# Two down projections, 1024 columns at a time, with seven products instead of eight in four of eleven pairs of chunks

## The chip, the cores and the metric

The kernel runs on one core of a Trainium2 chip. The metric is the device time of one execution in microseconds (us), which is to be low. The kernel before takes 1485.39 us (median of three runs, 1484.65 to 1486.05). All times below come from these runs, from the profile of one execution, or from questions put to that execution's trace.

## What is computed

The reference is one encoder layer over 256 tokens with 2048 features, all in float32. Cut to what matters here:

```python
x = x + merged @ w_out                       # attention branches, before
hf = rms_norm(x, ffn_norm)
g = dwconv_centred(hf @ w_ffn_gate, conv_w, conv_b)
x = x + (gelu(g) * (hf @ w_ffn_up)) @ w_ffn_down     # w_ffn_down: 5632 x 2048
gate_p = sigmoid(rms_norm(x, ple_norm) @ w_ple_gate)
x = x + gate_p * (p @ w_ple_proj)
return rms_norm(x, final_norm)
```

The product with `w_ffn_down` contracts over 5632 features, which are 44 chunks of 128. It is the product that the change touches.

## The kernel before, in words

**Precision.** Every float32 operand is split into a part `hi`, rounded to the matmul's format, and the rest `lo`. A product is three matmuls: hi by hi, hi by lo, lo by hi.

**The stream of weights.** All weights lie in HBM as one stream of blocks of 128x128, packed in the order of their use. A piece is 16 blocks (1 MB). `load` fetches a piece into one of three buffers `raw` by the DMA queue of SyncE (SP). `split_to` makes two splits of 8 blocks out of a piece: ScalarE (ACT) copies 128x1024 numbers of `raw` into `whi`, then VectorE (DVE) subtracts, `wlo` = `raw` - `whi`. There are four buffers of `whi` and four of `wlo`, so the split of a piece waits until TensorE (PE) is through with the split four earlier; the load of a piece waits until the last `wlo` of the piece three earlier is made. Each engine takes its instructions strictly in the order in which a scheduler wrote them.

**The work in order.** `_plan` lists jobs: the input projections (kinds q, k, v) with attention in between, the branch products (ga, gb, ba, bb), the output projection (o), and then, twice, one half of the gated MLP: 22 chunks f of the gate product (g) and the up product (u), followed by the down product (d0, d1) over these 22 chunks. After d1 come the two small products of the per-layer embedding (pp, two chunks each) and the gate of it (pg), and the final norm. The g and u products (`product`, `block`) hold a weight block still and stream the 256 tokens as hi and lo; the others (`wide_product`) hold 128 tokens still and stream 512 columns of weights. A d job in the kernel before is one quarter of the columns (512): for each of the 22 chunks, six matmuls, three for each half of the tokens, into two PSUM banks. `joined` then adds each bank to the residual `x` on DVE, and for d1 ACT takes squares for the next norm. `flip` transposes the residual on PE, 4 transposes per two chunks, and `gained` splits the result into `mov` (the operand `pl` of pg) with one ACT and one DVE instruction per chunk. The jobs pp and pg read what ACT puts into `ph`, and the last gain `lg`, which is fetched by a DMA of 1 MB.

**Work that is placed by a table.** `at` and `run_due` hang steps (flips, norms, fetches) on a job and a chunk number; the scheduler then places them in each engine's queue.

## Time and profile before

| | |
|---|---|
| median of three runs | 1485.39 us (1484.65 to 1486.05) |
| the profiled execution | 1485.03 us |
| its span, first to last instruction | 1483.1 us, so 1.9 us lie around it |
| granted TensorE clock | 0.998 |
| PE busy / DVE busy / ACT busy | 1472.1 / 975.9 / 729.4 us |
| read from HBM | 279.49 MB |

In the rows that follow, PE is TensorE, PEld its loading of the still operand, DVE VectorE, ACT ScalarE, SPq the DMA queue of SyncE. A row of a group has its busy time and the mean length of one instruction (in ns), and behind the bar's second part the idle time before it with what ended it. The timeline's rows have start and length in us, and in brackets how long the engine was idle before and what it waited for. A matmul's length there includes its latency: matmuls follow each other faster than that, so the pace of PE is read from the distance between starts, not from lengths. The same holds in a smaller way for DVE and ACT. d0 runs from 887.7 to 995 us of the span, d1 from 1256 to about 1374 us.

### The profile page before, as it was taken

Reading aid. Unit: us, or ns where it says so; the run is one execution under the profiler, and the core shown is the slowest. Engines: PE = TensorE matmul, PEld = TensorE weight load, DVE = VectorE, ACT = ScalarE, POOL = GpSimd, SP = SyncE. Lnnn points to the kernel's source line nnn. Section 1 sums busy time; section 2 is a strip of 40 time slices with the busy share of each in tenths; the row PEclk is TensorE's granted clock in tenths of the full one; section 3 lists DMA queues with packets and bytes.
Section 4 is the critical chain, followed back from the end, with each engine's and each line's share of the span. In section 5 each row is a group of like instructions: output and inputs, shape, how many; then the busy total and the mean of one; then the engine's idle time right before and its main releaser. Section 6 shows DMA issues by size and latency. Waiting matters only on the chain.

```text
span 1483.1 us, 19449 instructions
## 1 busy us (share of the span) xinstructions
PE 1472.1 (99%) x7618; PEld 1258.2 (85%) x7618; DVE 975.9 (66%) x1406; ACT 729.4 (49%) x1032; POOL 3.7 (0%) x9
## 2 busy tenths in 40 slices
PE   9999999999999999999999999999999999999997
PEld 8888888888888888888888888888888888888886
DVE  7686665655554555578888885447888887555565
ACT  7565444444444444554554554344555555444553
POOL 0000000000000000000000000000000000000000
PEclk9999999999999999999999999999999999999999
DMA  8744444446555555565555555555555555555552
GB/s 320 257 153 161 170 171 172 169 178 205 196 194 205 184 203 202 178 220 183 188 197 188 183 197 197 187 189 193 196 179 194 199 179 191 199 175 193 196 188 99
DMA packets 46375, 282.89 MB, mean 191 GB/s; under 512 B 5124, under 2 KB 9988, under 8 KB 14028
## 3 DMA queue, kind: packets, MB, share of 16 engines
q1 hardware_dynamic: 44268, 277.31, 52.3%
q10 hardware_dynamic: 2016, 4.33, 1.1%
q8 instruction: 60, 0.98, 0.3%
q14 instruction: 31, 0.25, 0.0%
HBM read 279.49 MB, written 2.14 MB: 190 GB/s over the span
## 4 chain that ended last, share of the span: by engine, by line
PE 97%; DVE 1%; ACT 0%; DMA 0%; issue 0%; POOL 0%; ACTq 0%; POOLq 0%; DVEq 0%
PE acc L202 28%; PE acc L225 17%; PE acc L226 17%; PE acc L227 17%; PE acc L203 14%; PE first L202 2%; PE first L203 1%; PE pt L483 0%; PE pt L608 0%; DVE wlo L192 0%; PE sp L442 0%; PE misc L498 0%; PE pt L629 0%; DMA x<-in_xt 0%; PE misc L429 0%; PE misc L430 0%
## 5 line engine op out<-in xcount | busy, mean ns | idle before, releaser
L192 DVE TENSOR_TENSOR wlo<-raw,whi 128x1024 fp32r<-128x1024 f32 (+1 forms) x519 | 632.2, 1218 | 467.3 <-ACT whi L191 465.7
L191 ACT ACTIVATE whi<-raw 128x1024 fp32r<-128x1024 f32 (+1 forms) x519 | 547.9, 1056 | 670.7 <-PE acc L227 355.2
L202 PE MATMUL acc<-mov,whi 128*128 128x512 f32 x1840 | 642.1, 394 | 0.0
L203 PE MATMUL acc<-mov,wlo 128*128 128x256 f32 x1840 | 512.9, 279 | 0.0
L202 PEld LDWEIGHTS acc<-mov,whi 128*128 128x128 f32 x1840 | 344.7, 187 | 77.5
L203 PEld LDWEIGHTS acc<-mov,wlo 128*128 128x128 f32 x1840 | 346.8, 188 | 0.5
L225 PE MATMUL acc<-whi,mov 128*128 128x512 f32 (+1 forms) x640 | 247.6, 387 | 0.0
L227 PE MATMUL acc<-whi,mov 128*128 128x512 f32 (+1 forms) x640 | 246.2, 385 | 0.0
L226 PE MATMUL acc<-wlo,mov 128*128 128x512 f32 (+1 forms) x640 | 246.2, 385 | 0.0
L225 PEld LDWEIGHTS acc<-whi,mov 128*128 128x128 f32 x640 | 120.8, 189 | 24.0 <-DVE wlo L192 0.8
L227 PEld LDWEIGHTS acc<-whi,mov 128*128 128x128 f32 x640 | 120.7, 189 | 24.0
L226 PEld LDWEIGHTS acc<-wlo,mov 128*128 128x128 f32 x640 | 120.8, 189 | 22.9
L225 PE MATMUL acc<-whi,act 128*128 128x512 f32 x352 | 137.5, 391 | 0.0
L227 PE MATMUL acc<-whi,act 128*128 128x512 f32 x352 | 137.0, 389 | 0.0
L226 PE MATMUL acc<-wlo,act 128*128 128x512 f32 x352 | 136.9, 389 | 0.0
L227 PEld LDWEIGHTS acc<-whi,act 128*128 128x128 f32 x352 | 66.1, 188 | 13.9
L225 PEld LDWEIGHTS acc<-whi,act 128*128 128x128 f32 x352 | 66.1, 188 | 13.6
L226 PEld LDWEIGHTS acc<-wlo,act 128*128 128x128 f32 x352 | 66.1, 188 | 13.2
L253 ACT ACTIVATE t<-acc 128x256 f32<-128x256 f32 x115 | 42.1, 366 | 0.0
L257 DVE TENSOR_TENSOR u<-acc,t 128x256 f32<-128x256 f32 x100 | 41.8, 418 | 0.0
L202 PE MATMUL first<-mov,whi 128*128 128x512 f32 x112 | 38.6, 397 | 0.2
L225 PE MATMUL acc<-whi,yab 128*128 128x512 f32 x96 | 37.3, 389 | 0.0
(144 smaller groups left out, 912.5 us busy)
## 6 DMA issues: line engine op xcount, KB each, us to landing
raw<-in_wts SPq DMA_DIRECT2D x251, 1024.0 KB, 4.8
raw<-in_wts SPq DMA_DIRECT2D x12, 512.0 KB, 7.2
x<-in_xrows ACTq DMA_DIRECT2D x8, 256.0 KB, 5.3
x<-in_xt SPq DMA_DIRECT2D x13, 128.0 KB, 6.7
mov<-hold SPq DMA_DIRECT2D x3, 514.0 KB, 6.6
mov<-hold SPq DMA_DIRECT2D x2, 768.0 KB, 6.9
mov<-in_last_gain ACTq DMA_DIRECT2D x1, 1024.0 KB, 5.7
out<-x ACTq DMA_DIRECT2D x2, 384.0 KB
```

The source lines that it names most:

```text
L191: nc.scalar.activation(hi, src, AF.Copy)
L192: nc.vector.tensor_tensor(lo, src, hi.bitcast(F32), op=ALU.subtract)
L202: nc.tensor.matmul(acc, hi[:, o, :], m, start=first, stop=False, skip_group_check=True)
L203: nc.tensor.matmul(acc[:, T:], lo[:, o, :], m[:, :T], start=False, stop=last, skip_group_check=True)
L225: nc.tensor.matmul(acc, xh, hi, start=(k == 0), stop=False)
L226: nc.tensor.matmul(acc, xh, lo, start=False, stop=False)
L227: nc.tensor.matmul(acc, xl, hi, start=False, stop=(k == n - 1))
L253: keep(nc.scalar.activation(t, acc[:, T:], AF.Copy, scale=scale))
L257: nc.vector.tensor_tensor(u, acc[:, :T], t, op=ALU.add)
```

## The change

Each half's down product becomes two jobs of 1024 columns instead of four of 512. With 256 tokens (two halves of rows, A1 and A2), two chunks of 128 features and 1024 columns (two halves of 512), a pair of chunks is a 2x2 by 2x2 product of quarters. For four of the eleven pairs (numbers 0 to 3 of `ORDER`, which alternates them with unsaved pairs: 4, 0, 5, 1, 6, 2, 7, 3, 8, 9, 10) the eight products of quarters are replaced by seven products of sums of quarters, in the variant with 15 additions. The other seven pairs are computed as before, into four of the seven banks.

- *Activations.* `add_up`, once per half after chunk 7 of the up product, forms four sums for all four saved pairs (four DVE instructions of 128x512) and splits them (two ACT and two DVE instructions of 128x1024). Chunks 0 to 7 are kept in float32 in `a32` for that.
- *Weights.* For a saved pair, `combine` forms four differences of the weights' quarters from the piece `raw` in the buffer `spare`: one DVE instruction of 128x1024 and two of 128x512. The piece then gives four splits instead of two: 8 blocks of `raw`, 8 of `spare`, 8 of `spare`, 4 of `raw`. The splits serve 6, 6, 6 and 3 matmuls; a split of an unsaved piece serves 12. `seven_product` asks for splits one further ahead than `wide_product`.
- *Spreading.* After the last saved pair, `spread_sums` takes p1 with one ACT instruction and, with eight DVE instructions of 128x512, adds p1, p5, p6 and p7 to the residual in the four places where they belong. p2, p3, p4 and c22 gather the unsaved pairs and are joined at the end of the job as before: four `joined` per job, in a row.
- *Banks.* The seven banks are all that PSUM has but one; the two jobs of a half swap the names, so that a job begins in banks that have long been read.
- *Memory and moves.* The large buffers are cut anew. The last gain is fetched in job pp 2 instead of at the beginning of d1. After the last d1 job, four flips instead of two are left, at pp 1, pp 2 (two) and pp 3.

The diff, cut to its core:

```diff
-        wide("d%d" % half, "w_ffn_down", half * FHALF, FHALF)
+        for c in range(2):
+            jobs.append(("d%d" % half, c, "w_ffn_down", tuple(range(8 * c, 8 * c + 8)), half * FHALF, FHALF))
...
+ORDER = [4, 0, 5, 1, 6, 2, 7, 3, 8, 9, 10]
+SAVED = 4
...
+        if isinstance(n, tuple) and len(n) == 8:
+            for m in ORDER:
+                if m < SAVED:
+                    _SEVEN.add(len(blocks))
+                blocks += [(name, k0 + 2 * m + e, c) for e in range(2) for c in n]
+            continue
...
+def _splits():
+
+    subs = [(int(a), n, None) for a, n in zip(np.cumsum([0, 1, 2, 4, 4]), (1, 2, 4, 4, 5))]
+    for a in range(PIECE, len(_BLOCKS), PIECE):
+        if a in _SEVEN:
+            subs += [(a, PIECE, part) for part in range(4)]
+        else:
+            subs += [(a + o, SUB, None) for o in range(0, PIECE, SUB)]
+    return subs
+
...
+            if part is not None:
+                src = combine(src, part)
+                n = src.shape[1]
...
+    def combine(b, part):
+
+        if part == 0:
+            state["turn"] = turn = 1 - state.get("turn", 1)
+            state["t"] = held["spare"][:, turn * PIECE * P:(turn + 1) * PIECE * P].rearrange("p (b n) -> p b n", n=P)
+            four = b.rearrange("p (q b) n -> p q (b n)", q=4)
+            t13 = state["t"][:, :8, :].rearrange("p (q b) n -> p q (b n)", q=2)
+            nc.vector.tensor_tensor(t13, four[:, 1::2], four[:, :2], op=ALU.subtract)
+            return b[:, 8:, :]
+        if part == 1:
+            t1, t2, t4 = (state["t"][:, c:c + 4, :] for c in (0, 8, 12))
+            nc.vector.tensor_tensor(t2, b[:, 12:, :], t1, op=ALU.subtract)
+            nc.vector.tensor_tensor(t4, b[:, 8:12, :], t2, op=ALU.subtract)
+            return state["t"][:, :8, :]
+        return state["t"][:, 8:, :] if part == 2 else b[:, :4, :]
 
     def block(acc, m, first, last, ahead=3):
...
+    def seven_product(i, still, sums, tags, done):
...
+        seen, uses = {}, {}
+        for m in ORDER:
+            for name in ("p2", "p3", "p4") + (("p1", "p5", "p6", "p7") if m < SAVED else ("p2", "p3", "p4", "c22", "c22")):
+                uses[name] = uses.get(name, 0) + 1
+
+        def step(name, pair, hi, lo):
+            xh, xl = pair
+            seen[name] = e = seen.get(name, 0) + 1
+            acc = of(name)
+            nc.tensor.matmul(acc, xh, hi, start=(e == 1), stop=False)
+            nc.tensor.matmul(acc, xh, lo, start=False, stop=False)
+            nc.tensor.matmul(acc, xl, hi, start=False, stop=(e == uses[name]))
+
...
+        k = 0
+        for m in ORDER:
+            b = state["at"]
+            s, _ = _SUB_OF[b]
+            if m < SAVED:
+                each = ([("p3", sums(m, 3), 0, 4), ("p2", a(2 * m + 1, 0), 0, 0)],
+                        [("p5", sums(m, 0), 1, 0), ("p7", sums(m, 2), 1, 4)],
+                        [("p6", sums(m, 1), 2, 0), ("p4", a(2 * m + 1, 1), 2, 4)],
+                        [("p1", a(2 * m, 0), 3, 0)])
+            else:
+                each = [[(name, a(2 * m + e, t), e, o) for name, t, o in (("p2", 0, 0), ("p3", 0, 4), ("p4", 1, 0),
+                                                                         ("c22", 1, 4))] for e in range(2)]
+            for e, steps in enumerate(each):
+                if m >= SAVED or e % 2 == 0:
+                    run_due(i, k)
+                    k += 1
+                for name, pair, part, o in steps:
+                    split_to(s + part + 4)
+                    hi, lo = (w[:, o:o + 4, :] for w in subs[s + part])
+                    step(name, pair, hi, lo)
+                del subs[s + part]
+            state["at"] = b + PIECE
+            if m == SAVED - 1:
+                done(bank)
+        return bank
 
     sc = ctx.enter_context(tc.tile_pool(name="sc", bufs=2))
 
@@ -334,11 +432,10 @@
...
+            f = n % FHALF
+            v = held["a32"][:, f, :] if f < 2 * SAVED else u
+            nc.vector.tensor_tensor(v, u, held.pop(("gelu", n)), op=ALU.mult)
+            halves(held["act"][:, f, :], v)
+            if f == 2 * SAVED - 1:
+                add_up()
...
+    def add_up():
+
+        a = held["a32"].rearrange("p (m e) (t n) -> p m e t n", e=2, t=2)
+        a11, a12, a21, a22 = a[:, :, 0, 0], a[:, :, 1, 0], a[:, :, 0, 1], a[:, :, 1, 1]
+        s = held["s32"]
+        nc.vector.tensor_tensor(s[:, 0], a21, a22, op=ALU.add)
+        nc.vector.tensor_tensor(s[:, 1], s[:, 0], a11, op=ALU.subtract)
+        nc.vector.tensor_tensor(s[:, 2], a11, a21, op=ALU.subtract)
+        nc.vector.tensor_tensor(s[:, 3], a12, s[:, 1], op=ALU.subtract)
+        hi, lo = held["shl"][:, 0], held["shl"][:, 1]
+        for c in (slice(0, 2), slice(2, 4)):
+            nc.scalar.activation(hi[:, c], s[:, c], AF.Copy)
+            nc.vector.tensor_tensor(lo[:, c], s[:, c], hi[:, c].bitcast(F32), op=ALU.subtract)
+
...
+    def spread_sums(n, bank):
+
+        q = [[res[:, t, (2 * n + c) * W4:(2 * n + c + 1) * W4] for c in range(2)] for t in range(2)]
+        u = held["ff"].tile([P, W4], F32, name="sq4")
+        v = held["ff"].tile([P, W4], F32, name="gate", bufs=2)
+
+        def add(dst, a, b):
+            nc.vector.tensor_tensor(dst, a, b, op=ALU.add)
+
+        nc.scalar.activation(u, bank["p1"], AF.Copy)
+        add(q[0][0], u, q[0][0])
+        add(u, bank["p6"], u)
+        add(v, bank["p7"], u)
+        add(u, bank["p5"], u)
+        add(q[1][0], v, q[1][0])
+        add(v, bank["p5"], v)
+        add(q[0][1], u, q[0][1])
+        add(q[1][1], v, q[1][1])
 
...
+        if kind == "g" and n == 0:
+            spare = held["spare"] = big.tile([P, KC * T], F32, name="spare", tag="b0", bufs=1)
+            held["a32"] = spare[:, :2 * SAVED * T].rearrange("p (k t) -> p k t", t=T)
+            held["s32"] = spare[:, 2 * SAVED * T:4 * SAVED * T].rearrange("p (e m n) -> p e m n", e=4, n=P)
+            held["shl"] = big.tile([P, 2, 4, SAVED, P], FR, name="shl", tag="b1", bufs=1)
...
-            spare = big.tile([P, 2 * KC * T], F32, name="mov")
-            held["lg"] = spare[:, 2 * D:3 * D]
-            nc.scalar.dma_start(held["lg"], last_gain)
...
-        if kind in ("o", "d1"):
-            dst, g = (held["hf"], 1) if kind == "o" else (held["pl"], 2)
-            for e, j in enumerate(((i + 1, 2), (i + 1, 4)) if n < QUARTERS - 1 else
-                                  ((i + 1, 9), (i + 1, 11)) if kind == "o" else ((i + 2, 0), (i + 3, 0))):
-                at(j, flip, 4 * n + 2 * e, dst, g)
+        if kind == "o":
+            for e, j in enumerate(((i + 1, 2), (i + 1, 4)) if n < QUARTERS - 1 else ((i + 1, 9), (i + 1, 11))):
+                at(j, flip, 4 * n + 2 * e, held["hf"], 1)
+        if kind == "d1":
+            for e, j in enumerate(((i + 2, 0), (i + 3, 0), (i + 3, 1), (i + 4, 1)) if n else
+                                  [(i + 1, k) for k in (17, 18, 19, 20)]):
...
-            held["ph"] = ff.tile([P, 2, QUARTERS, W4], F32, name="ph", tag="act")
+            end = ff.tile([P, 3 * QUARTERS, W4], F32, name="end", tag="act")
+            held["ph"] = end[:, :2 * QUARTERS].rearrange("p (t n) w -> p t n w", t=2)
+            held["lg"] = end[:, 2 * QUARTERS:].rearrange("p n w -> p (n w)")
         if kind == "pp" and n == 2:
+            keep(nc.scalar.dma_start(held["lg"], last_gain))
             nc.vector.tensor_scalar(held["half"], root(rowsums(held["ss2"]), 2), 0.5, None, op0=ALU.mult)
...
+        elif kind in ("d0", "d1"):
+            names = ("p2", "p3", "p4", "c22"), ("p1", "p5", "p6", "p7")
+            places = ("sp", "sp", "pt", "pt"), ("acc", "acc", "acc", "misc")
+            tags = {a: b for e in range(2) for a, b in zip(names[e], places[e ^ n])}
+            acc = seven_product(i, lambda k: held["act"][:, k, :], summed, tags, lambda bank: spread_sums(n, bank))
...
+        elif kind in ("d0", "d1"):
+            for name, t, c in (("p2", 0, 0), ("p3", 0, 1), ("p4", 1, 0), ("c22", 1, 1)):
+                joined(2 * n + c, t, acc[name], 1.0, held["ss2"] if kind == "d1" else None)
```

**Three places in the order of instructions.** The first is DVE at the down product d0. In the kernel before, the last rows of the up product and then the first quarter and a part of the second (`wlo<-raw,whi` is a weight split, `x<-acc,x` is `joined`):

```order
L597 TENSOR_TENSOR u<-u,c 128x256
L192 TENSOR_TENSOR wlo<-raw,whi 128x1024
L265 TENSOR_TENSOR act<-u,act 128x256
L192 TENSOR_TENSOR wlo<-raw,whi 128x1024 x9
L639 TENSOR_TENSOR x<-acc,x 128x512 x2
L192 TENSOR_TENSOR wlo<-raw,whi 128x1024 x11
```

Now, in the middle of the first job of 1024 columns; `spare<-raw` and `spare<-raw,spare` are `combine`, `wlo<-spare,whi` the split of its result:

```order
L218 TENSOR_TENSOR wlo<-raw,whi 128x1024 x3
L218 TENSOR_TENSOR wlo<-spare,whi 128x1024 x2
L229 TENSOR_TENSOR spare<-raw 128x1024
L218 TENSOR_TENSOR wlo<-raw,whi 128x512
L233 TENSOR_TENSOR spare<-raw,spare 128x512
L234 TENSOR_TENSOR spare<-raw,spare 128x512
L218 TENSOR_TENSOR wlo<-raw,whi 128x1024 x3
```

The three `wlo<-raw,whi` at the top are the two splits of an unsaved piece and the first of a saved one, the row x2 its second and third, and the 128x512 its fourth. The first difference of the next saved pair (`spare<-raw` 128x1024) stands ahead of that fourth split, and so ahead of the unsaved piece's splits that follow.

The second place is ACT between d1 and pg. Before (`sq` are the squares of `joined`, `ph<-acc` the evictions of pp, `mov<-pt,cl` the flips' splits):

```order
L644 ACTIVATE sq_11735,marks<-x 128x512
L644 ACTIVATE sq_11738,marks<-x 128x512
L601 ACTIVATE ph<-acc 128x512 x2
L269 ACTIVATE mov<-pt,cl 128x256
L191 ACTIVATE whi<-raw 128x1024
L269 ACTIVATE mov<-pt,cl 128x256
L601 ACTIVATE ph<-acc 128x512 x2
L269 ACTIVATE mov<-pt,cl 128x256
L191 ACTIVATE whi<-raw 128x1024
```

Now the same stretch, with `end<-acc` in the place of `ph<-acc`:

```order
L367 ACTIVATE mov<-pt,cl 128x256
L702 ACTIVATE end<-acc 128x512 x2
L876 DMA end<-in_last_gain 128x2048
L367 ACTIVATE mov<-pt,cl 128x256 x2
L702 ACTIVATE end<-acc 128x512
L367 ACTIVATE mov<-pt,cl 128x256 x2
L702 ACTIVATE end<-acc 128x512
L217 ACTIVATE whi<-raw 128x1024
L367 ACTIVATE mov<-pt,cl 128x256
L702 ACTIVATE end<-acc 128x512 x2
L217 ACTIVATE whi<-raw 128x1024
L367 ACTIVATE mov<-pt,cl 128x256
```

There are two more flips here than before, and the last weight split stands behind a flip's split and two evictions.

The third place is PE at the last flip. Before, with buffer numbers (`pw` is the operand of pp, `ident,x` a flip's transposes):

```order
L227 MATMUL acc_11764<-whi_11718,pw_10899 128x512
L608 MATMUL pt_11801<-ident_73,x_69 128x128 x4
L225 MATMUL acc_11799<-whi_11745,pw_10899 128x512
L226 MATMUL acc_11799<-wlo_11746,pw_10899 128x512
L227 MATMUL acc_11799<-whi_11745,pw_10899 128x512
L225 MATMUL acc_11800<-whi_11745,pw_10899 128x512
```

After these follow the rest of pp 2 and the whole of pp 3, 24 matmuls with `pw` between the last transposes and the first matmul of pg. Now:

```order
L268 MATMUL acc_12029<-wlo_11963,pw_11013 128x512
L745 MATMUL pt_12040<-ident_73,x_69 128x128 x4
L269 MATMUL acc_12029<-whi_11962,pw_11013 128x512
L267 MATMUL acc_12057<-whi_12001,mov_11010 128x512
L268 MATMUL acc_12057<-wlo_12002,mov_11010 128x512
L269 MATMUL acc_12057<-whi_12001,mov_11010 128x512
```

And at the point where the third split of pg is first used:

```order
L267 MATMUL acc_12057<-whi_12030,mov_11010 128x512
L268 MATMUL acc_12057<-wlo_12031,mov_11010 128x512
L269 MATMUL acc_12057<-whi_12030,mov_11010 128x512
L267 MATMUL acc_12057<-whi_12061,mov_11010 128x512
L268 MATMUL acc_12057<-wlo_12062,mov_11010 128x512
```

One matmul of pp is left between the transposes and pg, and from there to the first use of `wlo_12062` there are 14 matmuls: that one, twelve on two earlier splits, and one on `whi_12061`.

64 lines of the change are left out of this document (38 added, 26 removed).

## Prediction

> **What bounds the kernel now.** First the page: the span, the busy engines, the chain that ended last; then the waits, PE's own asked for apart.
>
> ```profile
> span 1483.1 us, 19449 instructions
> PE 1472.1 (99%) x7618; PEld 1258.2 (85%) x7618; DVE 975.9 (66%) x1406; ACT 729.4 (49%) x1032; POOL 3.7 (0%) x9
> PE 97%; DVE 1%; ACT 0%; DMA 0%; issue 0%; POOL 0%; ACTq 0%; POOLq 0%; DVEq 0%
> ```
> ```profile
> PE misc L158 <- DVE mhalf L153: 1.1, 1, 1.1
> ```
> ```profile
> DVE wlo L192 <- ACT whi L191: 465.7, 394, 2.4
> ACT whi L191 <- PE acc L227: 355.2, 226, 3.3
> ```
>
> PE is the chain: once started it never waits by its own rows, while the splits wait for PE to free buffers. So a matmul less is its pace less, as long as DVE, ACT and the loads keep ahead. How near they are is read by stretches: gate and up with its tail, then d0.
>
> ```profile
> 664.00:887.70 223.70, 223.70 (x1292) 197.22 (x1292) 183.38 (x324) 115.19 (x183) 0.00 (x0) 1.00 0.53 191
> 887.70:995.00 107.30, 107.30 (x475) 88.89 (x474) 53.39 (x51) 42.86 (x42) 0.00 (x0) 1.00 0.54 192
> ```
>
> After the stretch and its length come PE, PEld, DVE and ACT busy. In d0 DVE is busy for 53.39 of 107.30 us, half the time. That room is what the change spends. In gate and up 183.38 of 223.70 us are taken, and 40.3 us are free, 1.83 us per chunk f.
>
> **The pace of PE.** Two splits on ACT in d0, nine splits apart:
>
> ```profile
> 904.34 1.06 ACT L191 ACTIVATE whi<-raw 128x1024 fp32r<-128x1024 f32 x1 [1.66 <-PE acc L227]
> ...
> 928.82 1.06 ACT L191 ACTIVATE whi<-raw 128x1024 fp32r<-128x1024 f32 x1 [1.66 <-PE acc L227]
> ```
>
> 24.48 us / 9 = 2.72 us for the twelve matmuls of a split, 0.2267 us each.
>
> **What goes.** Two halves, two jobs each, four saved pairs per job, one product of three matmuls per pair: 48 matmuls, **48 x 0.2267 = 10.88 us**. Nothing else is taken off PE.
>
> **What DVE, ACT and the loads get.** Call an unsaved pair and the saved one behind it a round. PE needs 24 + 21 = 45 matmuls for it, 45 x 0.2267 = 10.20 us. What an added instruction costs is read where DVE has no gap:
>
> ```profile
> 1410.78 1.22 DVE L192 TENSOR_TENSOR wlo<-raw,whi 128x1024 fp32r<-128x1024 f32 x1
> 1411.92 1.29 DVE L655 TENSOR_TENSOR x<-x,mov 128x512 f32<-128x512 f32 x2
> 1413.12 1.22 DVE L192 TENSOR_TENSOR wlo<-raw,whi 128x1024 fp32r<-128x1024 f32 x1
> ```
> ```profile
> L371 DVE TENSOR_TENSOR squares<-squares,sq 128x1024 f32<-128x1024 f32 x3 | 3.7, 1222 | 0.0
> L655 DVE TENSOR_TENSOR x<-x,mov 128x512 f32<-128x512 f32 x6 | 3.9, 686 | 0.0
> L601 ACT ACTIVATE ph<-acc 128x512 f32<-128x512 f32 x8 | 4.7, 594 | 1.1 <-PE acc L227 0.7
> ```
>
> A 128x1024 lasts 1.22 us but the next starts after 1.14; two of 128x512 take 1.20 from start to start, 0.60 each. L371 (float32 in SBUF, 1.222 us) is the nearest row to the first difference of the weights, L655 (0.686 us) to the two smaller ones. DVE per round: 5 splits x 1.14 + 0.60 + differences 1.14 + 0.69 (the second of 512 waits for the first, so a whole length) + 0.60 = 8.7 us of 10.20. ACT, at the lengths of its rows: 5 x 1.06 + 0.59 = 5.9 us. Both fit, DVE at 86%. What remains is whether a single chain closes more slowly than PE. One does, almost: SP issues a load when the last `wlo` of the piece three earlier is made.
>
> ```profile
> SPq L175 <- DVE wlo L192: 686.3, 136, 7.5
> ```
> ```profile
> raw<-in_wts SPq DMA_DIRECT2D x15, 1024.0 KB, 4.8
> ```
>
> By the order of DVE in the change's rows, the second split of an unsaved piece frees the buffer into which the next saved piece but one lands; its first difference stands on DVE ahead of the fourth split of the saved piece before it, the two smaller differences, and both splits of the following unsaved piece, the second of which frees the next buffer. So from one such split to the next, one round: landing 4.8 + difference 1.14 + fourth split 0.60 + 0.69 + 0.60 + split 1.14 + split 1.22 to its end = 10.19 us, and about 0.03 us to issue. Against PE's 10.20 that is a tie: 0.02 us over, and with three such links in each of four jobs 12 x 0.02 = **0.24 us lost**. The upper end takes each DVE instruction at its whole length, 1.22 or 0.69: 10.56 us, 0.36 over, 12 x 0.36 = 4.3 us. The lower end is nothing lost, and no gain, since PE had no wait there to lose.
>
> Such a tie has no room for a late load, and there are late ones: this load, asked for alone, out of the fifteen above.
>
> ```profile
> raw<-in_wts SPq DMA_DIRECT2D x1, 1024.0 KB, 6.9
> ```
>
> It is 2.1 us late. A part of that is covered, because a split is made ahead. How long that takes after PE frees its buffer, the first matmul of d0 and the split that follows two splits later tell:
>
> ```profile
> 887.78 0.39 PE L225 MATMUL acc<-whi,act 128*128 128x512 f32 x1
> ```
> ```profile
> 893.52 1.06 ACT L191 ACTIVATE whi<-raw 128x1024 fp32r<-128x1024 f32 x1 [1.37 <-PE acc L227]
> ```
>
> PE is through with 24 matmuls at 887.78 + 5.44 = 893.22, and `whi` starts 0.30 later; 1.06 and 1.22 more make 2.6 us. In the new rounds the unsaved piece's first split waits for a buffer that a saved piece's first split frees, and PE then has 6 + 6 + 3 matmuls left, 3.4 us. So 0.8 us is covered and a late load costs 1.3 us. One of fifteen, for twelve loads: **12 / 15 x 1.3 = 1.0 us**; the ends are none and three late ones, 0 and 4 us.
>
> **Spreading and joining.** `spread_sums` is one ACT and eight DVE instructions, at most 8 x 0.69 = 5.5 us, while PE has three unsaved pairs, 72 x 0.2267 = 16.3 us. Six splits need 6.8 us of DVE, so 4.0 us are left, and the order puts splits between the additions. Its banks are wanted again only in the next job. `joined` is the same sixteen instructions, in fours: 2.4 us at once instead of 1.2, behind splits made ahead. I cost both at nothing; without that cover, 5.5 us per job.
>
> **Sums of activations.** Per half, 4 x 0.60 + 2 x 1.14 = 4.7 us on DVE in gate and up, which have 1.83 us free per chunk and splits made two ahead (16 matmuls each; 223.7 us / 44 products / 2 = 2.5 us a split, 5 us in all). Nothing; if the lead is already spent, up to 2 us per half. The first differences of the down product (2.4 us) fall into the last chunk of the same stretch under the same cover.
>
> **Between d1 and pg.** Here cover goes. Before, 24 matmuls lay between the last flip's transposes and pg; now one, and ACT has the flip's split, two evictions, then the weight split that pg's fifteenth matmul needs.
>
> ```profile
> 1380.39 0.60 PE L608 MATMUL pt<-ident,x 128*128 128x128 f32 x4
> ```
> ```profile
> 1381.08 0.47 ACT L269 ACTIVATE mov<-pt,cl 128x256 fp32r<-128x256 f32 x1
> 1381.44 1.06 ACT L191 ACTIVATE whi<-raw 128x1024 fp32r<-128x1024 f32 x1
> ...
> 1383.09 1.28 ACT L601 ACTIVATE ph<-acc 128x512 f32<-128x512 f32 x2 [0.22 <-PE acc L227]
> 1384.26 1.05 ACT L191 ACTIVATE whi<-raw 128x1024 fp32r<-128x1024 f32 x1
> ```
>
> From the end of the transposes (1380.99): 0.09 to the flip's split, 0.36 to the next start, 1.17 for two evictions, 1.06 for `whi`, 0.03, 1.22 for `wlo` = 3.93 us. PE has 14 x 0.2267 = 3.17. **0.76 us of waiting**, ends 0 and 2 (a second split late). The load of the last gain moves here too: 1 MB issued by ACT beside a load of weights. A load issued beside another transfer landed late,
>
> ```profile
> raw<-in_wts SPq DMA_DIRECT2D x1, 1024.0 KB, 7.5
> x<-in_xrows ACTq DMA_DIRECT2D x1, 256.0 KB, 5.3
> ```
>
> at 7.5 instead of 4.8. Pieces are loaded over one piece ahead (5.4 us), so nothing; at worst 2.7 us.
>
> **The sum.** 1485.03 - 10.88 + 0.24 + 1.0 + 0.76 = 1476.15, 8.9 us below the profiled execution. That execution lies 0.36 us below the median of the runs, so I forecast 1485.39 - 8.9 = **1476.5 us**.
>
> **Rivals.**
>
> *DVE does not overlap, so the round is longer than PE's.* The whole lengths give 4.3 us instead of 0.24: 1485.4 - 10.88 + 4.3 + 1.0 + 0.76 = **1480.6 us**. For it: it needs only 0.03 us more per instruction than I take, and whether an instruction waits for a signal in front of it changes that. Against it: the two starts 1.14 apart above. [...] Chance 0.14.
>
> *Loads land late round after round: slower.* The change issues loads unevenly, at the ends of splits that crowd together, and every round hangs on one landing. If the landing takes 6.9 us as in the late one, each round is 2.1 us over: 12 x 2.1 = 25.2, less the 0.8 us of cover once per job, 22 us, and the time is 1485.4 - 10.88 + 22 + 0.76 = **1497 us**. It decides from where 12 links cost the 10.1 us that remain of the saving: 0.84 + 0.27 of cover per link, landing at 5.9 us. For it: 7.5 above, and the chain has no slack. Against it: two loads that SP issued only 4.0 us apart, late in the span, of which the second landed as always:
>
> ```profile
> 1433.79 4.34 SPq L175 DMA_DIRECT2D raw<-in_wts  x2
> ```
> ```profile
> raw<-in_wts SPq DMA_DIRECT2D x1, 1024.0 KB, 4.8
> ```
>
> Chance 0.06.
>
> *The cover outside the rounds fails.* If `spread_sums` and the sums of activations stop PE for 2 us at each of six places, 2 us are lost at pg, and the last gain delays a load by 2.7 us, less the 0.76 already counted, 15.9 us would be lost; half of it, 8 us, gives 1476.5 + 8 = **1484.5 us**, no change. Against it: 4.0 us of room at each spreading. Chance 0.06. That the change does not do what it says I leave out: the order shows PE's matmuls in sevens.
>
> **How the numbers follow.** The forecast has 0.74, and the rivals 0.14, 0.06 and 0.06. A measurement of this kernel tells a change from none at about 0.2%, 3 us. Faster by over that, below 1482.4: the forecast and the first rival, 0.88. Within: the third, 0.06. Slower: the second, 0.06. The range goes from all 10.88 us saved and the runs' own 0.7 us below the median, 1473.8, to the first rival with one more late load, 1482.0; outside are the other two rivals.
>
> **What would show it.** PE: 48 matmuls of 512 fewer. PE's waits in the down product: about 1 us for `wlo`; tens of short ones, 0.4 us each, mean the first rival. DVE: waits for the load ahead of the first difference (`spare` from `raw`), 0.1 to 0.5 us; DVE busy in d0 for about 85% of a round. Loads: 4.8 us in d0; 5.9 or more prove the second rival. One wait of PE of about 0.8 us at pg's third split. I am wrong if PE's pace is not 2.72 us per twelve matmuls in the new jobs, or if PE waits at `add_up` or behind `spread_sums`.

## The result and the profile after

The changed kernel takes 1477.65 us (median of four runs, 1476.47 to 1479.64) against 1485.72 us for the kernel before in the same comparison (1484.65 to 1486.97). The ratio is 0.9949, 95% interval 0.9936 to 0.9961: faster by 0.5%, 8.1 us. The forecast was 1476.5 us, 8.9 us less.

The page of the changed kernel, the profiled execution of 1477.88 us:

```profile
span 1476.1 us, 19530 instructions
PE 1462.2 (99%) x7570; PEld 1248.4 (85%) x7570; DVE 1065.5 (72%) x1530; ACT 760.5 (52%) x1072; POOL 3.7 (0%) x9
```

7618 matmuls have become 7570, the 48 of the forecast. DVE has 1065.5 - 975.9 = 89.6 us more to do, and PE is still busy for 99% of the span. Nearly the same two stretches as before the change (they part at 887.5 us instead of 887.7), with PE, PEld, DVE and ACT busy behind each stretch and its length:

```profile
664.00:887.50 223.50, 223.50 (x1292) 197.06 (x1291) 188.68 (x333) 117.30 (x183) 0.00 (x0) 1.00 0.51 189
887.50:995.00 107.50, 106.69 (x472) 87.76 (x471) 92.56 (x104) 58.56 (x63) 0.00 (x0) 1.00 0.54 201
```

In d0 DVE is now busy for 92.56 of 107.50 us, 86%, and PE for the first time is not busy throughout: 0.81 us are missing. In gate and up nothing is missing, with the first half's `add_up` in it. What PE waited for, by its own rows:

```profile
PE acc L312 <- DVE wlo L218: 0.8, 2, 0.4
PE acc L268 <- DVE wlo L218: 0.5, 1, 0.5
PE acc L244 <- DVE mov L368: 0.3, 1, 0.3
```

Four waits where there were none, apart from the stretch before 50 us, which is taken up below. What such a wait costs is read from start to start, since the row's bracket holds less than the whole. The four places on PE's timeline, each with the matmul in front of it:

```profile
648.43 0.39 PE L244 MATMUL acc<-mov,whi 128*128 128x512 f32 x1
649.09 0.50 PE L244 MATMUL acc<-mov,whi 128*128 128x512 f32 x1 [0.27 <-DVE mov L368]
...
919.63 0.39 PE L311 MATMUL acc<-whi,act 128*128 128x512 f32 x1
920.45 0.50 PE L312 MATMUL acc<-wlo,act 128*128 128x512 f32 x1 [0.43 <-DVE wlo L218]
920.79 0.39 PE L313 MATMUL acc<-whi,act 128*128 128x512 f32 x1
...
977.48 0.39 PE L311 MATMUL acc<-whi,act 128*128 128x512 f32 x1
978.25 0.50 PE L312 MATMUL acc<-wlo,act 128*128 128x512 f32 x1 [0.38 <-DVE wlo L218]
...
1381.10 0.39 PE L267 MATMUL acc<-whi,mov 128*128 128x512 f32 x1
1382.00 0.50 PE L268 MATMUL acc<-wlo,mov 128*128 128x512 f32 x1 [0.52 <-DVE wlo L218]
```

Less the pace of 0.2267 us they cost 0.43, 0.59, 0.54 and 0.67 us. The matmul behind each of them then starts 0.34 us later instead of 0.23 (920.45 to 920.79), so each costs 0.11 us more, and the four together 2.67 us. The fifth difference stands ahead of everything that the change touches. The first matmul behind the first projection, on PE's timeline before:

```profile
45.27 1.03 PE L398 MATMUL misc<-oh,tb 32*20 32x512 f32 x2
```

and after:

```profile
46.52 1.03 PE L495 MATMUL misc<-oh,tb 32*20 32x512 f32 x2
```

That execution was 1.25 us late by then. Not all of it lasts: the first matmul of the first gate product, before and after:

```profile
642.31 0.39 PE L202 MATMUL acc<-mov,whi 128*128 128x512 f32 x1
...
642.99 0.39 PE L244 MATMUL acc<-mov,whi 128*128 128x512 f32 x1
```

So 0.68 us of it are left where the first of the four waits comes. The sum for the two profiled executions: -10.88 + 2.67 + 0.68 = -7.53 us, against spans of 1476.1 - 1483.1 = -7.0 us. Of the half microsecond that is left over, 0.2 us would be explained by the worth of the 48 matmuls that less_48 measures below; the rest stays open.

Where the two waits in the down product come from stands on DVE, two rounds of the first d0 job in a row:

```profile
904.62 1.23 DVE L229 TENSOR_TENSOR spare<-raw 128x1024 f32<-128x1024 f32 x1
905.76 0.69 DVE L218 TENSOR_TENSOR wlo<-raw,whi 128x512 fp32r<-128x512 f32 x1
906.36 0.69 DVE L233 TENSOR_TENSOR spare<-raw,spare 128x512 f32<-128x512 f32 x1
907.08 0.69 DVE L234 TENSOR_TENSOR spare<-raw,spare 128x512 f32<-128x512 f32 x1
907.69 3.58 DVE L218 TENSOR_TENSOR wlo<-raw,whi 128x1024 fp32r<-128x1024 f32 x3
911.19 1.22 DVE L218 TENSOR_TENSOR wlo<-spare,whi 128x1024 fp32r<-128x1024 f32 x1
913.44 1.23 DVE L218 TENSOR_TENSOR wlo<-spare,whi 128x1024 fp32r<-128x1024 f32 x1 [1.03 <-ACT whi L217]
916.10 1.23 DVE L229 TENSOR_TENSOR spare<-raw 128x1024 f32<-128x1024 f32 x1 [1.44 <-DMA raw<-in_wts]
```

This is the prediction's chain, instruction by instruction: first difference (L229), fourth split (128x512), two small differences (L233, L234), split, split. The spacings are 1.14, 0.60, 0.72, 0.61, and the next load could go at 910.05, when the second split of the row of three ended. The next first difference comes 916.10 - 904.62 = 11.48 us later instead of 10.20; without its wait of 1.44 us for the load it would have been 10.04. PE's wait at 920.45, 0.59 us, is what the lead of the splits did not cover of the 1.44: 0.85 us were covered.

### The profile page after: what moved, and what is told of

It is laid out like the page before. It is cut to its first block, busy times and chain, and to the rows that moved or that the text cites. A ratio compares the mean times of both kernels' runs of the same rounds, so it can differ in the third digit from the quotient of the medians.

```text
span 1476.1 us, 19530 instructions
## 1 busy us (share of the span) xinstructions
PE 1462.2 (99%) x7570; PEld 1248.4 (85%) x7570; DVE 1065.5 (72%) x1530; ACT 760.5 (52%) x1072; POOL 3.7 (0%) x9
## 5 line engine op out<-in xcount | busy, mean ns | idle before, releaser
L218 DVE TENSOR_TENSOR wlo<-raw,whi 128x1024 fp32r<-128x1024 f32 (+2 forms) x519 | 622.1, 1201 | 355.6 <-ACT whi L217 352.4
L217 ACT ACTIVATE whi<-raw 128x1024 fp32r<-128x1024 f32 (+2 forms) x519 | 541.1, 1043 | 605.5 <-PE acc L269 224.9
L268 PE MATMUL acc<-wlo,mov 128*128 128x512 f32 (+1 forms) x512 | 196.5, 384 | 0.5 <-DVE wlo L218 0.5
L267 PE MATMUL acc<-whi,mov 128*128 128x512 f32 (+1 forms) x512 | 196.8, 385 | 0.0
L269 PE MATMUL acc<-whi,mov 128*128 128x512 f32 (+1 forms) x512 | 196.4, 384 | 0.0
L267 PEld LDWEIGHTS acc<-whi,mov 128*128 128x128 f32 x512 | 96.7, 189 | 19.3 <-DVE wlo L218 0.8
L269 PEld LDWEIGHTS acc<-whi,mov 128*128 128x128 f32 x512 | 96.7, 189 | 18.8
L312 PE MATMUL acc<-wlo,act 128*128 128x512 f32 x272 | 106.3, 391 | 0.8 <-DVE wlo L218 0.8
L311 PE MATMUL acc<-whi,act 128*128 128x512 f32 x272 | 106.1, 390 | 0.0
L313 PE MATMUL acc<-whi,act 128*128 128x512 f32 x272 | 105.9, 389 | 0.0
L311 PEld LDWEIGHTS acc<-whi,act 128*128 128x128 f32 x272 | 51.1, 188 | 10.7
L267 PE MATMUL acc<-whi,merged 128*128 128x512 f32 x128 | 50.6, 396 | 0.0
L269 PE MATMUL acc<-whi,merged 128*128 128x512 f32 x128 | 49.9, 390 | 0.0
L268 PE MATMUL acc<-wlo,merged 128*128 128x512 f32 x128 | 49.8, 389 | 0.0
L217 ACT ACTIVATE whi<-spare 128x1024 fp32r<-128x1024 f32 x32 | 33.7, 1054 | 27.0 <-PE acc L313 26.2
```

The source lines that it names most:

```text
L217: nc.scalar.activation(hi, src, AF.Copy)
L218: nc.vector.tensor_tensor(lo, src, hi.bitcast(F32), op=ALU.subtract)
L267: nc.tensor.matmul(acc, xh, hi, start=(k == 0), stop=False)
L268: nc.tensor.matmul(acc, xh, lo, start=False, stop=False)
L269: nc.tensor.matmul(acc, xl, hi, start=False, stop=(k == n - 1))
L311: nc.tensor.matmul(acc, xh, hi, start=(e == 1), stop=False)
```

## The experiments

**Only the matmuls (less_48).** The kernel before with 48 matmuls left out, the second half-split of chunks 7 and 15 in each quarter of the down product, so that part of the product is missing:

```diff
-            if k < n - late:
+            if n == FHALF and k in (7, 15):
+                pass
+            elif k < n - late:
```

> The kernel before, with the products of chunks 7 and 15 and the second half of the tokens left out of each down job: 8 jobs x 2 x 3 = 48 matmuls fewer, and nothing added; its down product is incomplete by that. Theory: the ceiling of the change, 1485.7 - 10.9 = 1474.8 us, no wait of PE. Rival (a matmul left out is worth less than its pace, because PE waits for splits instead): PE shows waits in the down product, 1477 us or more.

Measured: 1475.08 us (1474.33 to 1475.32) against 1485.76, ratio 0.9926 (0.9913 to 0.9938): -10.7 us. The 48 matmuls are worth 0.2225 us each, within 2% of the pace read from the splits, and everything else in the change together costs some 2.6 us (1477.65 - 1475.08, two comparisons whose kernel before agrees within 0.04 us), or 3.5 us by the repeat below, which saved 7.2 us.

**Dose (none_saved, two_saved, five_saved).** The same code with 0, 2 or 5 saved pairs; with 0 only the regrouping into 1024 columns and what was moved with it is left. With 5 the sums of activations have to be cut over other buffers.

```diff
-ORDER = [4, 0, 5, 1, 6, 2, 7, 3, 8, 9, 10]
-SAVED = 4
+ORDER = [0, 1, 2, 3, 4, 5, 6, 7, 8, 9, 10]     # none_saved
+SAVED = 0
+ORDER = [2, 0, 3, 1, 4, 5, 6, 7, 8, 9, 10]     # two_saved
+SAVED = 2
+ORDER = [5, 0, 6, 1, 7, 2, 8, 3, 4, 9, 10]     # five_saved
+SAVED = 5
```

> The change without its point: jobs of 1024 columns, four joined at once, the new banks, memory, flips and place of the last gain, but all eleven pairs by eight products. Theory (the time follows the number of matmuls, all else costs at most the wait at the gate product): PE does as many matmuls as before, so 1485.7 plus about 0.7 us for the wait at the gate product, 1486.4 us. Rival (the gain comes from the regrouping, not from fewer products): most of the 8 us stays, 1478 to 1481 us.

> Two saved pairs per job instead of four, alternating with unsaved ones. Theory: 24 matmuls fewer than before, 24 x 0.2267 = 5.44 us, against 0.7 us at the gate product and 0.3 us in the rounds: 1485.7 - 4.4 = 1481.3 us, half way. Rival (spreading and sums cost a fixed price per job, which four pairs pay off and two do not): 1484 us or more. Rival (regrouping): as with four, 1478 us.

> Five saved pairs per job, in the order 5, 0, 6, 1, 7, 2, 8, 3, 4, 9, 10, so that two saved pairs stand together once per job; the sums and their splits lie in other buffers for it. Theory: 60 matmuls fewer than before, 13.6 us, against 0.7 us at the gate product, 1.2 us of late loads and up to 1.5 us where the two stand together and in gate and up: 1475.5 us. Rival (VectorE is at its end with four): each further pair loses what it saves, 1477.7 us or more, with PE waiting for splits after the two that stand together.

Measured against 1485.76: none 1487.14 us (1486.78 to 1487.67; ratio 1.0008, 1.0 to 1.0017), two 1481.36 (1480.89 to 1482.47; 0.997, 0.996 to 0.9981), where 1481.3 was expected, five 1477.22 (1476.21 to 1479.9; 0.994, 0.9926 to 0.9953). A saved pair takes away 12 matmuls, 2.72 us. Going from none to two gave 5.8 us of 5.4; from two to four, the changed kernel, 3.7 of 5.4; from four to five 0.4 of 2.7. So the regrouping by itself costs 1.4 us, 0.7 more than expected: its profile has the waits at the first gate product and at pg, and none in the down product. The first two pairs are had in full, and with two the profile has no wait of PE in the down product either. Of the next two some two thirds are had. The fifth brought nothing that stands out of the scatter, since the runs with four and with five each lie 3 us apart: there the expectation of 1475.5 us failed. PE's waits in the profile with five, which is of the slowest of its five runs (1479.9), show two reasons:

```profile
PE acc L312 <- DVE wlo L218: 2.1, 2, 1.5
PE acc L244 <- DVE x L775: 1.0, 1, 1.0
```

The first is the wait for a split behind a late load again, longer now; the second is taken up under spaced, below.

**Saved pairs in a row (in_a_row).** The first four pairs saved one behind the other, nothing unsaved between them:

```diff
-ORDER = [4, 0, 5, 1, 6, 2, 7, 3, 8, 9, 10]
+ORDER = [0, 1, 2, 3, 4, 5, 6, 7, 8, 9, 10]
```

> The four saved pairs first, one behind the other, then the seven others. PE has 21 x 0.2267 = 4.76 us for a saved pair, DVE 3 x 1.14 + 0.60 + 1.14 + 0.69 + 0.60 = 6.45 us. Theory (DVE must keep pace with PE within the four buffers): PE waits 1.7 us per saved pair, 6.8 us per job, of which the lead of about 3 us is taken off: 4 x 3.5 = 14 us, 1491 us, slower than before, and DVE without a gap over the saved pairs. Rival (only the sum over a job counts, where DVE needs about 50 us of 54): 1477.7 us as with the alternating order.

Measured: 1488.70 us (1487.57 to 1489.07) against 1486.22, ratio 1.0016 (1.0007 to 1.0025): the whole saving is gone. DVE between two first differences:

```profile
895.84 1.23 DVE L229 TENSOR_TENSOR spare<-raw 128x1024 f32<-128x1024 f32 x1
...
902.18 1.23 DVE L229 TENSOR_TENSOR spare<-raw 128x1024 f32<-128x1024 f32 x1
```

And PE's waits in d0 there:

```profile
PE acc L311 <- ACT whi L217: 1.5, 3, 0.6
PE acc L312 <- DVE wlo L218: 1.1, 4, 0.4
```

6.34 us for a saved pair, for which PE needs 21 x 0.2267 = 4.76. DVE has no idle time in between. The direction is the theory's, the size is smaller, 1488.7 for 1491. So the unsaved pair between two saved ones is what pays for the differences.

**More work for DVE (extra_difference).** The last small difference is computed twice:

```diff
             nc.vector.tensor_tensor(t4, b[:, 8:12, :], t2, op=ALU.subtract)
+            nc.vector.tensor_tensor(t4, b[:, 8:12, :], t2, op=ALU.subtract)
```

> The second small difference of the weights is computed twice in each saved pair: 16 DVE instructions of 128x512 more, 0.60 to 0.69 us each. The scheduler then sets the two small differences behind the splits of the unsaved pair. Theory (DVE has 1.5 us to spare in a round; what made PE wait was the chain through the load, which has one small difference less now): no slower, 1477 to 1478 us, without waits for the load that reach PE. Rival (DVE is what PE waits for): 16 x 0.6 = 9.6 us more, 1487 us.

Measured: 1478.30 us (1477.62 to 1480.4), ratio 0.9949 (0.9934 to 0.9964), the changed kernel's own ratio. Sixteen more instructions on DVE cost nothing that shows, so DVE's sum of work is not what limits. The expectation also said that no wait for a load would reach PE, and that failed: PE waits once in d0, 1.05 us at 977.82, behind a load of 6.6 us. But the tie of the chain was not tested by it: the scheduler placed the small differences anew, with splits in between,

```profile
906.42 0.68 DVE L233 TENSOR_TENSOR spare<-raw,spare 128x512 f32<-128x512 f32 x1
907.02 1.22 DVE L218 TENSOR_TENSOR wlo<-raw,whi 128x1024 fp32r<-128x1024 f32 x1
908.16 0.68 DVE L234 TENSOR_TENSOR spare<-raw,spare 128x512 f32<-128x512 f32 x1
```

and the added one (L235) behind the split that frees the buffer, out of the chain.

**A buffer of its own for the saved pieces (own_buffer).** A saved piece is loaded into a fourth buffer, used by saved pieces alone:

```diff
-            raws[r] = wpool.tile([P, PIECE, P], F32, name="raw", bufs=3)
+            own = r * PIECE in _SEVEN
+            raws[r] = (held["ff"] if own else wpool).tile([P, PIECE, P], F32, name="raw", tag="own" if own else "raw", bufs=1 if own else 3)
...
-            load_all(r + 3)
+            load_all(r + 4)
```

> The pieces of the saved pairs have a buffer of their own beside the three, so that no difference waits for a load that an unsaved split has to free. The scheduler then sets the first difference directly ahead of the first split of its pair, and the others between the splits, as late as they can be. Theory (the place of the differences in DVE's queue is what keeps PE fed: they must run while splits wait for PE): each saved pair's four splits now stand behind 1.14 + 0.69 + 0.60 us of differences when PE is near, with 0.8 us of cover, so about 1.2 us lost per saved pair, 16 x 1.2 = 20 us, 1497 us. Rival (only the load's chain makes PE wait): the 1.1 us of waits in the down products go, 1476.5 us.

Measured: 1497.96 us (1496.96 to 1498.19), ratio 1.008 (1.0063 to 1.0096), 20 us above the changed kernel. One buffer for every saved piece means that its load waits until the fourth split of the saved piece before is done, and DVE's rows in d0 show it:

```profile
DVE spare L230 <- DMA raw<-in_wts: 12.5, 6, 2.6
```

12.5 us of waiting for loads in d0 against 2.8 in the changed kernel, 2.1 us each time, and short waits of PE all over the saved pairs. The 1497 us that were expected were met in part by luck: they were reckoned from the place of the differences in DVE's queue, at 1.2 us per saved pair, and what DVE's rows show is a wait for the load. Since the order on DVE changed too, this run does not part the two. A chain through the load that is too long by some 2 us per round costs the 20 us of the second rival; what the rival lacked was a reason for loads to be that late.

**Loads made late (late_loads).** A small load into the same buffer ahead of each saved piece's:

```diff
+        if r * PIECE in _SEVEN:
+            nc.sync.dma_start(raws[r][:, a:a + 1, :], wts[r].rearrange("p (b n) -> p b n", n=P)[:, a:a + 1, :])
```

> In front of the load of each saved piece (eight rows of loads in four jobs, sixteen pieces in all) SP issues a small load of 128x128 into the same buffer, which the large one must wait for: the large one lands about 2 us later than it is asked for, 6.8 us instead of 4.8. Everything else is computed as in the changed kernel, but the scheduler, which knows of the small load, puts the first difference behind the fourth split on DVE and the small differences between the next splits. Theory: the prediction's chain was a tie only because it held the fourth split and two more behind the difference; in the order that the scheduler now writes the chain is 6.8 + 1.14 + 1.14 + 1.22 = 10.3 us against 10.2, so at most 12 x 0.1 us more and a wait or two where a load is later still: 1477.5 to 1480 us. Rival: the second rival of the prediction as it stood, every round about 2 us over, 1494 to 1498 us, with a wait of PE of about 2 us in each of twelve rounds.

Measured: 1477.76 us (1476.48 to 1479.65) against 1485.61, ratio 0.9949 (0.9936 to 0.9961). The small load takes its 2.0 us,

```profile
raw<-in_wts SPq DMA_DIRECT2D x3, 1024.0 KB, 4.9
raw<-in_wts SPq DMA_DIRECT2D x1, 64.0 KB, 2.0
```

(loads asked for from 930 to 943 us), and yet PE does not wait once in either d job. In the order that the scheduler then wrote, the first difference (918.48) comes behind the fourth split (915.73) and a split, and the small ones later still. The edit changes two things, landing and order, so it says only this: two more us of landing are affordable in an order that holds nothing behind the difference; it does not price the order of the changed kernel.

**The same kernel again (again).**

> The changed kernel as it is, nothing edited, timed a second time beside the three others. If the 8.1 us below the kernel before belong to the change, it gives 1477 to 1479 us again. Its profile tells which waits of PE belong to the program and which to one execution: the wait at the third split of pg (0.68 us) and the one at the first gate product (0.43 us) follow from an order of instructions and must stand in it within 0.1 us; the two of 0.5 to 0.6 us in d0, if they come from single late loads, move to other places or are missing; the first transposes, which started 1.24 us later than in the profile before, start where the first loads happen to land, so anywhere from 45.7 to 48 us. If instead the two waits in d0 come from the length of the chain through the load, they stand at the same products again.

Measured: 1478.41 us (1477.9 to 1481.82) against 1485.61, ratio 0.9957 (0.9945 to 0.997). So it saved 7.2 us, and the 8.1 of the first comparison is the better of two. Its waits of PE stand at 648.81, 920.17, 978.29 and 1382.00 us of the span, with 0.42, 0.58, 0.86 and 0.67 us: all four in the same places. For the two in d0 I had expected other places if late loads were the cause, and the same places if it was the length of the chain. That rule was wrong: they recur, and yet the same loads are late again. DVE waits 1.44 and 1.38 us for them in the first profile, 1.43 and 1.71 in the repeat. The one asked for at about 967.7 us, in the DMA view from 966 to 975 us of the changed kernel:

```profile
q8 instruction: 1, 0.02, 0.7%
...
raw<-in_wts SPq DMA_DIRECT2D x1, 1024.0 KB, 6.1
```

and the repeat:

```profile
q8 instruction: 1, 0.02, 0.6%
...
raw<-in_wts SPq DMA_DIRECT2D x1, 1024.0 KB, 6.3
```

A load of 4.8 us takes 6.1 and 6.3. The first line names what falls into the same window: a packet of 0.02 MB on a queue called instruction. More on this below.

**Last gain early, flips earlier (flips_early, gain_flips).** The first moves one flip of the last half a product earlier, the second also takes the last gain back to where the kernel before loaded it, in a buffer of its own:

```diff
-            for e, j in enumerate(((i + 2, 0), (i + 3, 0), (i + 3, 1), (i + 4, 1)) if n else
+            for e, j in enumerate(((i + 2, 0), (i + 2, 1), (i + 3, 0), (i + 3, 1)) if n else
...
+            held["lg"] = ff.tile([P, D], F32, name="lg")                       # gain_flips
+            nc.scalar.dma_start(held["lg"], last_gain)                         # gain_flips
...
-                keep(nc.scalar.dma_start(held["lg"], last_gain))               # gain_flips
```

> The last four flips at pp 1 and pp 2 instead of pp 1, pp 2 and pp 3, so that 18 or more matmuls lie between the last transposes and the third split of the gate product. Theory: the wait at that split, 0.7 us, shrinks to 0.4 or less; nothing else changes, 1477.3 us. Rival (the wait comes from ACT having too much in all, not from the place of the last flip): the wait stays at 0.7 us or moves to another split.

> The changed kernel with the last gain in a buffer of its own, loaded where the kernel before loaded it, and the flips of the last half one product earlier. Theory: pg's wait of 0.68 us falls to 0.2 to 0.4, because ACT has the flip's split done before the last product of d1 ends and issues no load there; the rest stays, and the time is 0.3 to 0.7 us below the changed kernel of the same batch, which these rounds can hardly tell from nothing. Rival: the load moved to the end of d1 did cost a late load of weights there, and more than 1 us comes back.

Measured: flips_early 1479.45 us (1478.53 to 1481.16), ratio 0.9956 (0.9941 to 0.9971); gain_flips 1479.26 (1477.28 to 1480.94), 0.9957 (0.9944 to 0.9969), against 1478.41 for the repeat beside it. The wait at pg fell to 0.39 us in the first and is gone in the second, at 1381.19, 1381.42 and 1381.65:

```profile
1381.19 0.39 PE L268 MATMUL acc<-wlo,mov 128*128 128x512 f32 x1
1381.42 0.40 PE L269 MATMUL acc<-whi,mov 128*128 128x512 f32 x1
1381.65 0.41 PE L267 MATMUL acc<-whi,mov 128*128 128x512 f32 x1
```

The mechanism is as expected; the gain of 0.3 to 0.7 us is not seen in the times, which lie 1 us higher if anything, inside their own scatter of 3 us. No version here is measurably better than the changed kernel.

**A looser round (spaced).**

```diff
-ORDER = [4, 0, 5, 1, 6, 2, 7, 3, 8, 9, 10]
+ORDER = [4, 0, 5, 6, 1, 7, 2, 8, 3, 9, 10]
```

> The order of the pairs in both jobs of a half changed from 4,0,5,1,6,2,7,3,8,9,10 to 4,0,5,6,1,7,2,8,3,9,10: two unsaved pairs behind the first saved one, so that one link of the chain of each job has 69 matmuls of PE behind it instead of 45, and the lead that a late load ate can be made up there. The same 48 matmuls are saved. Theory: the rounds of 10.2 us stand at a tie and lose only to single late loads, so a looser round saves at most those 0.5 to 1.1 us: 1476.5 to 1478 us, within 1 us of the changed kernel. Rival: rounds cost what the sums over the whole program hide (spreading behind three unsaved pairs, now behind four with the splits ahead), and the time moves by over 2 us either way.

Measured: 1478.64 us (1478.52 to 1478.91), ratio 0.9953 (0.9939 to 0.9967). That is above the 1476.5 to 1478 us that were expected, and no better than the repeat. The waits in the middle of d0 are gone, though one of 0.46 us stands in d1, and a new one stands where d0 ends, on DVE and on PE:

```profile
1003.35 2.47 DVE L776 TENSOR_TENSOR x<-acc,x 128x512 f32<-128x512 f32 x4
```

and

```profile
1004.18 0.47 PE L244 MATMUL acc<-mov,whi 128*128 128x512 f32 x1 [1.01 <-DVE x L776]
```

Only two unsaved pairs, 48 x 0.2267 = 10.9 us of PE, are left behind the last saved one. The additions of `spread_sums` then end late, the four of `joined` stand behind them, and the next job waits 1.17 us for the bank. With three pairs, as in the changed kernel, it does not wait. This is the cover of the prediction's third rival, and where it ends.

## Why the prediction was right, point by point

**PE as the chain, 48 x 0.2267.** Right: 48 matmuls fewer, and alone they are worth 10.7 us by less_48.

**The round and its tie, 0.24 us; late loads, 1.0 us.** Together 1.24 us; the profiles show 1.13 and 1.44 from start to start, and 0.22 more with what follows the two waits. The chain has the instructions and, to 0.1 us, the spacings of the forecast, and the cover of 0.8 us is there: DVE waited 1.44 and 1.38 us where PE waited 0.59 and 0.54. That the sum came out is in part luck, for the terms fell otherwise. Rounds whose load is punctual cost nothing, and all of the loss hangs on two late loads, both in d0; in d1 DVE waited for three loads, 0.6 us at most, and PE for none. That twelve rounds lose alike was wrong. A late load cost 0.5 to 0.9 us, not 1.3, as it took 6.1 to 6.3 us where its landing is on record, and not 6.9. And late loads were taken for chance, one in fifteen; the repeat shows that they come at the same loads again.

**pg, 0.76 us.** Right: 0.67 in both profiles, at its third split, and it shrinks when the flips stand earlier.

**Spreading, joining, sums of activations: nothing.** Right for this order: no wait of PE there. It has no pair to spare: spaced and five_saved, with two unsaved pairs behind the last saved one, waited 1.2 us at the end of d0.

**The last gain's load, nothing.** Half right. No load was late for it at pp. But it stood in ACT's queue at the end of the output projection before, and with it gone ACT's order there is another. On DVE this is seen as follows, before:

```profile
646.62 0.48 DVE L270 SCALAR_TENSOR_TENSOR mov<-pt,cl,mov 128x256 fp32r<-128x256 f32 x1 [1.10 <-ACT mov L269]
647.76 0.48 DVE L270 SCALAR_TENSOR_TENSOR mov<-pt,cl,mov 128x256 fp32r<-128x256 f32 x1 [0.66 <-ACT mov L269]
...
648.71 1.23 DVE L192 TENSOR_TENSOR wlo<-raw,whi 128x1024 fp32r<-128x1024 f32 x1
```

and after:

```profile
647.42 1.22 DVE L218 TENSOR_TENSOR wlo<-raw,whi 128x1024 fp32r<-128x1024 f32 x1
648.56 0.87 DVE L368 SCALAR_TENSOR_TENSOR mov<-pt,cl,mov 128x256 fp32r<-128x256 f32 x2
```

ACT now makes its half of the weight split ahead of its half of the flips. That does not make ACT's flips late: the first starts at 646.85 instead of 646.11, hardly more than the 0.68 us by which everything is later here. But on DVE the split of weights now stands ahead of the flips' second half, which starts 1.94 us later than before, and the first gate product waits 0.43 us for `mov`. This is the term that the forecast missed; it stood in the order, at a place that I did not look at, a job ahead of the change. That the gain's load leaving ACT's queue is what changed the order is argued, not shown: gain_flips issues it early again, at another place in ACT's queue, and keeps the wait.

**The start.** Not forecast: 1.25 us in the profile after, 0.97 in the repeat, of which 0.68 and 0.40 us are left at the first gate product. The instructions there are the same; first loads land at other times. The rest is made up between 270 and 310 us of the span, where the lag of PE's matmuls, counted off against those before, falls from 1.16 to 0.69 us in the profile after; what makes it up stays open. It stays open whether this is the program or the execution: less_48, close kin of the kernel before, and own_buffer, kin of the changed one, started within 0.25 us of the kernel before, the others 0.8 to 2.3 us later.

**The rivals.** The first, no overlap on DVE, is refuted: the instruction behind a first difference starts 1.14 us after it, at a length of 1.23, and the one behind the fourth split 0.60 after it at 0.69; of the differences only L234, which reads what L233 writes, takes the 0.72. The 0.03 us per instruction that the prediction names for this rival do not come out of its rows: from 1.14 to 1.22 and from 0.60 to 0.69 it is 0.08 and 0.09. The Trainium skill, "VectorE: DVE Perf Modes", section "The DRAIN you can't avoid", says that the next operation does not start until the pipe is empty, and adds that one which is not held starts earlier. The 1.14 and 0.60 us agree with what it adds. The second did not happen, since most loads in d0 took 4.7 to 4.9 us although they were issued 3.1 to 9.8 us apart; own_buffer, 20 us slower by 2.1 us of waiting per round, agrees with its price. The third did not happen in this order.

For the profiled execution the sum was 1.7 us too good (1476.15 for 1477.88): 0.68 us are the start, 0.54 the first gate product with what follows its wait, some 0.1 the other waits, and some 0.4 stay open. For the medians it was 0.8 us too good, and 1.7 for the repeat.

## What to carry to other kernels

A saving on the engine that sets the end is had in full only up to the point where the longest chain beside it ties with it: here the first two pairs brought all of their 2.7 us each, the next two about two thirds, the fifth nothing that can be told from the scatter. Write that chain down instruction by instruction, from the event that frees a buffer to the next such event; an engine that is busy for 86% carried 16 more instructions for nothing, and a load that could start only behind another piece's last split cost 20 us. And after moving a load look at every queue that it left, not only at the one that it joins.

## What the runs showed that I had not expected

**Late loads sit where code is fetched.** The page counts the packets of queue q8:

```profile
q8 instruction: 59, 0.97, 0.2%
```

0.97 MB in 59 packets, about 16 KB each. Two loads of the first d0 job, each with its stretch cut into 40 slices. The first, a punctual one (899.7 to 906.0 us of the changed kernel):

```profile
GB/s 520 312 520 312 208 208 260 156 156 260 52 312 364 156 260 416 416 364 520 364 468 312 520 312 416 156 364 52 0 0 0 0 0 0 0 0 0 0 0 0
...
raw<-in_wts SPq DMA_DIRECT2D x1, 1024.0 KB, 4.8
```

The second, a late one (909.8 to 916.1 us):

```profile
GB/s 416 416 416 416 104 0 0 52 260 208 208 52 52 104 312 260 416 260 572 312 520 260 520 364 468 364 416 312 156 104 52 52 0 52 0 52 0 0 0 0
...
q8 instruction: 1, 0.02, 1.7%
```

The first is over in slice 28. The second has moved its bulk by slice 30, and then single packets trickle for six slices more, 0.9 us; no view tells what held them up. It is the load for which DVE waited 1.44 us. Counted over the loads of 1 MB in all fourteen profiles from 660 to 1380 us, as far as their landing is on record (it is for 1361 of 1824): of 253 loads with such a packet of 16 KB on q8 within 4.5 us of their issue, 84 took over 5.3 us; of 1108 without, 18. In d0 alone, 887 to 997 us, it is 17 of 30 and 6 of 177. In d0 of the changed kernel the packets come 27 to 31 us apart; 27.9 us are 123 matmuls with 123 loads of the still operand, 246 instructions. The Trainium skill, "Runtime: NRT & Kernel Launch", section "Instruction fetch mechanics", gives blocks of 16 KiB with 256 instructions, fetched by each engine's own queue, and calls the cost mostly hidden. Size and rate agree with these rows. If the fetch delays the load, then a load that is waited for at a tie is where its cost is not hidden; but that is argued from the coincidence: no run moved the fetch alone.

**An edit for an experiment is scheduled anew.** One instruction more (extra_difference), one small load more (late_loads) or one buffer more (own_buffer) made the scheduler place the differences differently, which hid the cost that was to be measured or mixed with it. Each such run had to be read from its own order on DVE before its time meant anything.
